# Two projections per matmul: 512-wide token-major projections, their weight loads on ScalarE's queue, four and four PSUM banks

## The chip, the cores and the metric

The kernel runs on one core of one Trainium2 chip. The metric is the device time of one execution in microseconds (us); a kernel is timed in several runs and the median counts. TensorE does matrix products into PSUM (eight banks of 2 KB per partition, 512 float32 columns each), VectorE and ScalarE do elementwise work and empty PSUM, GpSimd does elementwise work on SBUF alone, and SyncE (SP) issues most of the DMAs.

## What is computed

One decoder layer in float32 over 2048 tokens of width 1024. Every token is RMS-normalised and goes through one input projection; its columns feed four mLSTM heads (q and k of 128, v, o and z of 256 columns each) and eight gated DeltaNet heads (q, k, v and a gate z of 128 columns each); one output projection, a residual and a final RMSNorm follow.

```python
def reference(x, attn_norm, w_in, ...):
    h = rms_norm(x, attn_norm[l])
    proj = jnp.einsum('bsd,dp->bsp', h, w_in[l])
    (mq, mk, mv, mo, mz, mi, mf, gqkv, gz, gb, ga) = jnp.split(proj, split_points, axis=-1)
    h_m = mlstm_chunkwise(q_m, k_m, v_m, i_pre, f_pre)
    h_m = h_m * lax.rsqrt(jnp.mean(h_m * h_m, axis=-1, keepdims=True) + EPS)
    y_m = merge_heads(h_m) * m_out_norm[l] * jax.nn.sigmoid(mo) * jax.nn.silu(mz)
    qkv = jax.nn.silu(causal_depthwise_conv(gqkv, g_conv[l]))
    o_g = gated_delta_chunkwise(l2_norm(q), l2_norm(k), v, log_alpha, beta)
    o_g = o_g * lax.rsqrt(jnp.mean(o_g * o_g, axis=-1, keepdims=True) + EPS) * g_out_norm[l]
    y_g = merge_heads(o_g) * jax.nn.silu(gz)
    x = x + jnp.einsum('bsm,md->bsd', jnp.concatenate([y_m, y_g], axis=-1), w_out[l])
    return rms_norm(x, final_norm)
```

## The kernel before

**Segments and windows.** The 2048 tokens are worked on in four segments of `T` = 512, each in four chunks of 128 (`NCH`). A segment has eight windows: P0, M0, P1, M1, ... P3, M3 (`ORDER`; the last segment ends P2, P3, M2, M3). A P window projects two DeltaNet heads (`g_proj`), an M window one mLSTM head (`m_proj`).

**Projections.** Each weight group of 256 columns and its activations are split into a high and a low part, and every product is three matmuls (high-high, high-low, low-high). `proj_fm` (lines 348 to 358) is feature-major: the stationary operand is a 128x128 piece of weight, 512 tokens stream by; it serves q, k and the DeltaNet's q, k, v. `proj_tm` (lines 384 to 393, matmuls in `tm_step`, lines 360 to 365) is token-major: the stationary operand is a 128x128 piece of activations, and the 256 columns of one weight group stream by; it serves v, o and z of an mLSTM head (`pt_mv`, `pt_mo`, `pt_mz`) and the DeltaNet gate (`pt_gz`). A token-major group is four chunks of 8 x 3 matmuls, each chunk into a bank of its own.

**PSUM.** Three banks (`psj`, line 95) serve the projections, five (`psc`, line 96) everything else. An M window's v is emptied by ScalarE (high part, line 532) and VectorE (low part `vlo`, line 540), its z by ScalarE (tanh) and VectorE (lines 549 to 552).

**Weights.** SBUF holds ten units of 512 KB (half of a group's high or low part). In the first segment `split_w` loads the raw weights, splits them and keeps both parts in DRAM; later segments load them back from there. `next_w` fetches the following group's four units each time a group begins (line 161, on SP's queue). That queue works in order, and also carries the small transfers of the other streams: y rows out (lines 671, 1021), broadcast rows in (561, 750), the DeltaNet's 32x32 blocks through DRAM (841, 845, 856, 860).

**What runs beside the projections.** TensorE's order is written out by hand (`tc.manual_schedule`): `window` walks through a projection's steps (the filler) and at given fractions of the window puts in one step of another stream: `g_prep` (products of k and q, `kk`), `g_level` (block inverses: `zp`, `fp`, `zq`, `fq`), `g_chain` (per chunk `sp`, `vq`, then `su` and `op`) and `m_chunks` (per chunk `nd` and `up`). A window's length `WIN` is 41.6 us of filler; `LVP`, `CHP`, `CHM` hold the fractions. The other engines' order comes from a scheduler with priorities (`tc.high_priority`). In the first segment the projections use unnormalised activations (`raw`), and the outputs are scaled by `fm_out` (line 367).

**mLSTM key transposes.** `m_chunks` needs k token-major. Except for one head of the last segment, `to_tokens` (line 499) does it with 16 VectorE transposes of 32-row blocks per head (line 504).

Of the kernel before, what the change touches and what calls it, by code (L numbers as in the profile page):

```python
# [17 lines left out]
P = 128  # L18
# [11 lines left out]
LVP = (0.26, 0.3, 0.34, 0.4, 0.45)  # L30
# [3 lines left out]
CHM = (0.03, 0.11, 0.28, 0.45, 0.53, 0.7, 0.87, 0.95)  # L34
MW, MPR, VPR = ((0.07, 0.85), 200, 200)
# [23 lines left out]
MT = ((1, 1, 1, 1), (1, 1, 1, 1), (1, 1, 1, 0))  # L59
# [10 lines left out]
def hybrid_layer(  # L70
# [24 lines left out]
    psj = ctx.enter_context(tc.tile_pool(name="psj", bufs=3, space=PSUM))  # L95
    psc = ctx.enter_context(tc.tile_pool(name="psc", bufs=5, space=PSUM))
# [54 lines left out]

    def unit(ncol, dt, nm):
        return wp.tile([P, HK, ncol], dt, tag="wu", name=nm, bufs=10)

    def load_w(key, src, ncol, nm, between=None):

        if key in parts_d:
            his, los = ([unit(ncol, F32R, f"{p_}_{nm}_{i}") for i in range(2)] for p_ in ("whi", "wlo"))
            for i in range(2):
                for part, t_ in enumerate((his[i], los[i])):  # L160
                    nc.sync.dma_start(t_.bitcast(F32), parts_d[key][part, i])
            return his, los
        return split_w(key, src, ncol, nm, between)

    def split_w(key, src, ncol, nm, between):
# [18 lines left out]
        kept = parts_d[key] = ypool.tile([2, 2, P, HK, ncol], F32, tag=f"wd{nm}", name=f"wd{nm}")  # L184
        for i in range(2):
            for part, t_ in enumerate((his[i], los[i])):
                nc.sync.dma_start(kept[part, i], t_.bitcast(F32))
        return his, los

    wloads = []  # L190
    for seg in range(NSEG):
        for kind, n in ORDER_LAST if seg == NSEG - 1 else ORDER:
            for i in range(4) if kind == "M" else (3, 1, 0, 2) if n == 0 else (1, 0, 2, 3):
                nm, key = f"{kind}{seg}_{n}_{i}", (kind, n, i)
                if kind == "M":
# [7 lines left out]
    def prefetch_w(between=None):  # L203
        if wloads:
            wready.append(load_w(*wloads.pop(0), between))
# [38 lines left out]
    def rms_first():  # L244
        pc = psc.tile([P, T], F32, tag="cp", name="rcp0")[:, 0:NCH]
# [102 lines left out]
    def proj_fm(w, c0, nm, done):  # L348

        hi, lo = w  # L350
        ps = psj.tile([P, T], F32, tag="pj", name=f"pf_{nm}")
        for k in range(KT):
            nc.tensor.matmul(ps, lhsT=hi[k // HK][:, k % HK, c0:c0 + P], rhs=hh[k], start=(k == 0), stop=False)  # L353
            nc.tensor.matmul(ps, lhsT=hi[k // HK][:, k % HK, c0:c0 + P], rhs=hl[k], start=False, stop=False)  # L354
            nc.tensor.matmul(ps, lhsT=lo[k // HK][:, k % HK, c0:c0 + P], rhs=hh[k], start=False, stop=(k == KT - 1))  # L355
            if k == KT - 1:
                done(ps)
            yield 0.65

    def tm_step(ps, w, t, k):  # L360
        hi, lo = (p_[k // HK][:, k % HK, :] for p_ in w)
# [5 lines left out]
    def fm_out(dst, ps, scale=None):  # L367
# [16 lines left out]
    def proj_tm(w, nm, done, scaled=True):  # L384

        n = w[0][0].shape[-1]
        for t in range(NCH):
            ps = psj.tile([P, T], F32, tag="pj", name=f"pt_{nm}_{t}")[:, 0:n]
            for k in range(KT):
                tm_step(ps, w, t, k)  # L390
                if k == KT - 1:
                    tm_done(ps, t, done, scaled)
                yield 0.33

    def proj_tm_first(w, nm, done):

        n = w[0][0].shape[-1]
        pss = [psc.tile([P, T], F32, tag="cp", name=f"pt_{nm}_{t}")[:, 0:n] for t in range(NCH)]
        for k in range(KT):
            for t in range(NCH):  # L400
                tm_step(pss[t], w, t, k)
            if k == KT - 1:
# [105 lines left out]
    def m_proj(seg, n, r):  # L508
        s_ = f"{seg}_{n}"
        w = next_w()  # L510
# [6 lines left out]
        yield from proj_fm(w, 0, f"mq{s_}",  # L517
                           lambda ps: fm_out(qT, ps, DK ** -0.5))
        yield from proj_fm(w, P, f"mk{s_}", lambda ps: fm_out(kT, ps))
        w = next_w()  # L520
# [7 lines left out]
        def keep_v(ps, t):  # L528
# [12 lines left out]
        yield from proj_tm(w, f"mv{s_}", keep_v, False)  # L541
        w = next_w()
        yield from proj_tm(w, f"mo{s_}", lambda ps, t: nc.scalar.activation(
            G[:, t, :], ps, AF.Tanh, scale=rs0h[:, t:t + 1] if raw[0] else 0.5), False)
# [859 lines left out]
```

## Time and profile before

| | |
|---|---|
| median of 3 runs | 2281.76 us (2275.52 to 2284.42) |
| the profiled execution | 2285.25 us, span 2283.5 us |
| TensorE matmuls busy | 2210.1 us, 97% of the span, 14798 instructions |
| VectorE busy | 1842.6 us, 81% |
| ScalarE busy | 861.8 us, 38% |
| GpSimd busy | 797.3 us, 35% |
| mean granted TensorE clock | 0.985 of full speed |
| DMA | 409.19 MB, mean 179 GB/s |

The profile comes from one execution of the program, taken by the hardware profiler. Busy times of one engine overlap where its instructions are pipelined: a matmul's recorded duration is longer than the distance to the next one's start, so TensorE's pace is read from starts. "Idle before" is the time an engine stood still ahead of an instruction, with the instruction that released it.

### The profile page before, as it was taken

The page shows a single profiled execution, that of the slowest core. Times are in us where ns is not written, and L with a number is a line of the kernel's source. Part 1 is how long each engine was busy: PE and PEld are TensorE (multiplying, and loading weights), DVE is VectorE, ACT ScalarE, POOL GpSimd, SP SyncE. Part 2 cuts the span into 40 slices and gives each one's busy share as a digit, 9 for nine tenths or more (in the row PEclk, how much of TensorE's full clock was granted, in tenths as well). Part 3 has the DMA queues.
Part 4 walks back from the last instruction along what each step waited for, and adds up shares of the span by engine and source line. Part 5 has one row for each costly group of instructions (what it writes and reads, how often), then busy time and mean ns, then how long its engine had stood idle before and what let it go on. Part 6 is the DMA issues. An engine that isn't in the chain of part 4 may idle for free.

```text
span 2283.5 us, 41793 instructions
## 1 busy us (share of the span) xinstructions
PE 2210.1 (97%) x14798; PEld 1963.8 (86%) x14798; DVE 1842.6 (81%) x5168; ACT 861.8 (38%) x2289; POOL 797.3 (35%) x1220
## 2 busy tenths in 40 slices
PE   8899999989999999999999999999999999999998
PEld 7779898987989898988898989898988997788787
DVE  7988888788897979888979798788757737878784
ACT  5445454535343434352424243524244334111111
POOL 4657565652120202521212114212111115555543
PEclk9999999999999999999999999999999999999999
DMA  8767676764536464655454546544546545222321
GB/s 273 265 236 252 231 242 240 255 216 157 193 135 213 138 212 159 224 167 182 162 187 163 176 169 237 178 152 166 184 168 209 192 152 162 80 96 92 102 84 65
DMA packets 183322, 409.19 MB, mean 179 GB/s; under 512 B 51736, under 2 KB 84632, under 8 KB 183112
## 3 DMA queue, kind: packets, MB, share of 16 engines
q1 hardware_dynamic: 182392, 405.74, 52.4%
q8 instruction: 116, 1.90, 0.3%
q14 instruction: 94, 0.77, 0.1%
q10 hardware_dynamic: 720, 0.79, 0.1%
HBM read 309.68 MB, written 96.90 MB: 178 GB/s over the span
## 4 chain that ended last, share of the span: by engine, by line
PE 62%; DVE 25%; DMA 5%; ACT 4%; issue 2%; POOL 2%; SPq 0%; POOLq 0%; ACTq 0%; DVEq 0%
PE po L1260 5%; PE po L1259 5%; PE po L1258 5%; DVE tb L850 3%; DVE xb L854 3%; DVE kw L504 2%; PE pf_gv L355 2%; PE pf_gv L353 2%; PE pf_gv L354 2%; PE pt_gz L365 2%; PE pf_gq L353 2%; PE pt_gz L363 2%; PE pt_gz L364 2%; PE pt_mo L363 2%; PE pt_mo L364 2%
## 5 line engine op out<-in xcount | busy, mean ns | idle before, releaser
L1219 DVE STREAM_TRANSPOSE ytt<-yl 32x256 f32<-32x256 f32 x448 | 195.3, 436 | 45.3 <-POOL ylo L1187 39.2
L1016 POOL TENSOR_TENSOR gms<-gms,nhalf 128x2 f32<-128x2 f32 x64 | 46.7, 729 | 395.8 <-DVE gms L1014 386.5
L850 DVE TENSOR_TENSOR tb<-xb,lbt 128x248 f32<-128x248 f32 (+30 forms) x496 | 170.1, 343 | 17.8 <-DMA lbt<-l_d 5.0
L854 DVE TENSOR_TENSOR xb<-xb,tb 128x248 f32<-128x248 f32 (+30 forms) x496 | 167.7, 338 | 13.2
L363 PE MATMUL pt_mv<-whi_M,hh 128*128 128x256 f32 x512 | 152.7, 298 | 21.7 <-DVE vlo L540 14.6
L363 PE MATMUL pt_mz<-whi_M,hh 128*128 128x256 f32 x512 | 149.7, 292 | 7.6 <-DVE tz L550 7.5
L363 PE MATMUL pt_gz<-whi_P,hh 128*128 128x256 f32 (+1 forms) x512 | 149.7, 292 | 1.8 <-ACT whi_P L179 1.5
L364 PE MATMUL pt_mv<-wlo_M,hh 128*128 128x256 f32 x512 | 148.6, 290 | 0.1
L365 PE MATMUL pt_mv<-whi_M,hl 128*128 128x256 f32 x512 | 148.5, 290 | 0.0
L363 PE MATMUL pt_mo<-whi_M,hh 128*128 128x256 f32 x512 | 148.4, 290 | 0.0
L365 PE MATMUL pt_gz<-whi_P,hl 128*128 128x256 f32 (+1 forms) x512 | 146.7, 286 | 0.4 <-DVE hl L342 0.2
L364 PE MATMUL pt_gz<-wlo_P,hh 128*128 128x256 f32 (+1 forms) x512 | 146.4, 286 | 0.4 <-DVE wlo_P L182 0.4
L365 PE MATMUL pt_mz<-whi_M,hl 128*128 128x256 f32 x512 | 145.1, 283 | 0.0
L364 PE MATMUL pt_mz<-wlo_M,hh 128*128 128x256 f32 x512 | 145.1, 283 | 0.0
L364 PE MATMUL pt_mo<-wlo_M,hh 128*128 128x256 f32 x512 | 144.2, 282 | 0.0
L365 PE MATMUL pt_mo<-whi_M,hl 128*128 128x256 f32 x512 | 144.2, 282 | 0.0
L363 PEld LDWEIGHTS pt_mv<-whi_M,hh 128*128 128x128 f32 x512 | 101.4, 198 | 25.1 <-DVE vlo L540 16.0
L1267 ACT ACTIVATE jkf<-xr 128x512 f32<-128x512 f32 (+1 forms) x33 | 20.4, 619 | 271.5 <-DVE xr L1265 148.4
L1258 PE MATMUL po<-woh,yh 128*128 128x512 f32 (+1 forms) x297 | 114.6, 386 | 1.5 <-ACT yh L1185 1.5
L1260 PE MATMUL po<-woh,ylo 128*128 128x512 f32 (+1 forms) x297 | 114.9, 387 | 0.1
L1259 PE MATMUL po<-wol,yh 128*128 128x512 f32 (+1 forms) x297 | 114.3, 385 | 0.0
L182 POOL TENSOR_TENSOR wlo_M<-wraw_M,whi_M 128x256 fp32r<-128x256 f32 x128 | 98.4, 801 | 40.6 <-ACT whi_M L179 40.6
(407 smaller groups left out, 7541.7 us busy)
## 6 DMA issues: line engine op xcount, KB each, us to landing
whi_M<-wdM SPq DMA_DIRECT2D x96, 512.0 KB, 4.0
wlo_M<-wdM SPq DMA_DIRECT2D x96, 512.0 KB, 5.5
whi_P<-wdP SPq DMA_DIRECT2D x90, 512.0 KB, 4.7
wlo_P<-wdP SPq DMA_DIRECT2D x90, 512.0 KB, 6.0
wraw_M<-in_wg_dram SPq DMA_DIRECT2D x32, 512.0 KB, 5.8
wdM<-whi_M SPq DMA_DIRECT2D x32, 512.0 KB, 2.9
wdM<-wlo_M SPq DMA_DIRECT2D x32, 512.0 KB, 5.0
wraw_P<-in_wg_dram SPq DMA_DIRECT2D x30, 512.0 KB, 5.7
```

The lines of the kernel that those rows point to most:

```text
L182: eng.tensor_tensor(lo[:, ks, :], raw_[:, ks, :], hi[:, ks, :].bitcast(F32), op=ALU.subtract)
L353: nc.tensor.matmul(ps, lhsT=hi[k // HK][:, k % HK, c0:c0 + P], rhs=hh[k], start=(k == 0), stop=False)
L363: nc.tensor.matmul(ps, lhsT=hh[k][:, ts], rhs=hi, start=(k == 0), stop=False)
L364: nc.tensor.matmul(ps, lhsT=hh[k][:, ts], rhs=lo, start=False, stop=False)
L365: nc.tensor.matmul(ps, lhsT=hl[k][:, ts], rhs=hi, start=False, stop=(k == KT - 1))
L850: nc.vector.tensor_tensor(tb[:, :, 0:n], xb[:, :, i:i + 1].broadcast_to([P, 8, n]), lbt[:, i:i + 1, i + 1:32].broadcast_to([P, 8, n]), op= ...
L854: nc.vector.tensor_tensor(xs, xs, tb[:, :, 0:n], op=ALU.subtract)
L1016: nc.gpsimd.tensor_tensor(ms, ms, nhalf[:, 0:2], op=ALU.pow)
L1219: nc.vector.transpose(ytt[32 * b:32 * b + 32, :, 32 * a:32 * a + 32], y3[32 * a:32 * a + 32, :, 32 * b:32 * b + 32])
L1258: nc.tensor.matmul(ps, lhsT=yh, rhs=woh, start=(k == 0), stop=False)
L1259: nc.tensor.matmul(ps, lhsT=yh, rhs=wol, start=False, stop=False)
L1260: nc.tensor.matmul(ps, lhsT=ylo, rhs=woh, start=False, stop=(k == 15))
```

## The change

Five things change together.

- **Wide token-major projections** (`proj_tm_wide`). From the second segment on, o and z of an mLSTM head are projected together, 512 columns per matmul: two chunks at a time, each into a whole bank. For the DeltaNet gates of P1 to P3 (in the last segment of P1 alone) the gate leaves the P window and is projected in the M window that follows, together with v (`both`). The M window then begins with that pair, q and k come second. The fillers are 31.0 and 52.0 us long in such windows (`WINP`, `WINM`), with fractions of their own (`LVW`, `CWP`, `CWM`); the P window holds 4 chain steps instead of 5, the M window 9 instead of 8.
- **Weight units from ScalarE's queue.** From the second segment on, units are loaded by `pump`, called where the program frees a unit (`freed`), from ScalarE's queue; a wide group has eight units of two k-rows by 512 columns. The first segment's copies in DRAM are laid out 512 wide for the pairs.
- **Banks.** `psj` 4 instead of 3, `psc` 4 instead of 5. `rms_first` takes its bank from `psj`.
- **First segment's key transposes** go to TensorE (`MT`): 16 more transposes there, and where the products are split (`fast`) both parts are made from PSUM.
- **First segment's feature-major outputs** are scaled by one kind of VectorE instruction, with priority 200 (`VPR`).

```diff
-LVP = (0.26, 0.3, 0.34, 0.4, 0.45)
+NU = 10
+LVP, LVW = (0.26, 0.3, 0.34, 0.4, 0.45), (0.2, 0.24, 0.29, 0.34, 0.41)
 CHP = (0.42, 0.46, 0.63, 0.71, 0.88)
 CHM = (0.03, 0.11, 0.28, 0.45, 0.53, 0.7, 0.87, 0.95)
+CWP = (0.44, 0.5, 0.7, 0.82)
+CWM = (0.01, 0.15, 0.22, 0.36, 0.5, 0.57, 0.71, 0.85, 0.92)
...
-MT = ((1, 1, 1, 1), (1, 1, 1, 1), (1, 1, 1, 0))
+MT = ((0, 0, 0, 0), (1, 1, 1, 1), (1, 1, 1, 0))
...
-    psj = ctx.enter_context(tc.tile_pool(name="psj", bufs=3, space=PSUM))
-    psc = ctx.enter_context(tc.tile_pool(name="psc", bufs=5, space=PSUM))
+    psj = ctx.enter_context(tc.tile_pool(name="psj", bufs=4, space=PSUM))
+    psc = ctx.enter_context(tc.tile_pool(name="psc", bufs=4, space=PSUM))
...
+    ring = {"free": NU}
+    coming = []
+    def pump():
+        while coming and ring["free"] > 0:
+            w = coming[0]
+            at, src = w.due.pop(0)
+            t_ = w.units[at] = unit_(w.rows, w.n, F32R, f"w{at[0]}_{w.nm}_{at[1]}")
+            nc.scalar.dma_start(t_.bitcast(F32), src)
+            ring["free"] -= 1
+            if not w.due:
+                wready.append(coming.pop(0))
+    def freed(n):
+        ring["free"] += n
+        if not wloads:
+            pump()
...
+    WIDE = [[("M", n, 2), ("M", n, 3)] for n in range(4)] + [[("P", n, 3), ("M", n, 1)] for n in range(1, 4)]
+    def wide_z(seg, n):
+        return seg > 0 and n > 0 and not (seg == NSEG - 1 and n > 1)
...
+    def proj_tm_wide(w, nm, done):
+        for t0 in range(0, NCH, 2):
+            pss = [psj.tile([P, T], F32, tag="pj", name=f"pt_{nm}_{t0 + i}") for i in range(2)]
+            for k in range(KT):
+                for i in range(2):
+                    tm_step(pss[i], w, t0 + i, k)
+                    if t0 and i and k % 2:
+                        freed(2)
+                    if k == KT - 1:
+                        done(pss[i], t0 + i)
+                    yield 0.65
...
-        elif scale is None:
-            nc.vector.tensor_tensor(dst, ps, rbc0, op=ALU.mult)
         else:
-            nc.vector.scalar_tensor_tensor(dst, ps, scale, rbc0, op0=ALU.mult, op1=ALU.mult)
+            with tc.high_priority(VPR):
+                nc.vector.scalar_tensor_tensor(
+                    dst, ps, 1.0 if scale is None else scale, rbc0, op0=ALU.mult, op1=ALU.mult)
...
+        def gates(ps, t):
+            nc.scalar.activation(G[:, t, :], ps[:, 0:256], AF.Tanh, scale=0.5)
+            gate(ps[:, 256:512], t)
+        if wide_z(seg, n):
+            z_gate = g_gate(seg, n, rp, None)
+            def both(ps, t):
+                z_gate(ps, t)
+                keep_v(ps[:, 256:512], t)
+            yield from proj_tm_wide(next_w(), f"mv{s_}", both)
...
-        if fast or by_dve(MT, seg, h):
+        if by_dve(MT, seg, h) or not fast:
+            kw = sm.tile([P, NCH, P], F32, tag="kw", name=f"kw{s_}", bufs=1)
+        if by_dve(MT, seg, h):
             to_tokens(kT, kw)
...
+            if fast:
+                kw = ktp.rearrange("p (c f) -> p c f", c=NCH)
...
-    WIN = 41.6
+    WIN, WINP, WINM = 41.6, 31.0, 52.0
```

## Rows read from the trace of the kernel before

**Rows 1.** The page's first part: busy time, share and instructions of each engine.

```profile
PE 2210.1 (97%) x14798; PEld 1963.8 (86%) x14798; DVE 1842.6 (81%) x5168; ACT 861.8 (38%) x2289; POOL 797.3 (35%) x1220
```

**Rows 2.** Who waited for whom, TensorE: us in total, times, longest.

```profile
PE pt_mv L363 <- DVE vlo L540: 14.6, 7, 3.4
PE pt_mz L363 <- DVE tz L550: 7.5, 5, 3.1
PE vq L982 <- DVE vr L976: 4.8, 2, 3.8
...
PE pt_mv L363 <- DVE mk L375: 4.0, 2, 3.5
...
PE pt_mv L363 <- DVE vlo L537: 3.1, 2, 3.0
PE zp L910 <- DVE dmz L904: 3.0, 2, 1.8
PE sp L973 <- DVE ua L832: 2.4, 1, 2.4
```

**Rows 3.** Six stretches at half clock: busy by engine, PEclk, DMA share, GB/s.

```profile
1043.80:1050.60 6.80, 6.18 (x29) 6.18 (x30) 6.56 (x23) 3.54 (x10) 2.84 (x4) 0.50 0.49 152
...
sum 23.90, PE 23.02 PEld 22.73 DVE 19.78 ACT 8.75 POOL 5.32; mean PE 3.84 PEld 3.79 DVE 3.30 ACT 1.46 POOL 0.89
```

**Rows 4.** Timeline of TensorE, first and last of 62 matmuls of 256 columns.

```profile
702.97 0.28 PE L364 MATMUL pt_mo<-wlo_M,hh 128*128 128x256 f32 x1
...
710.22 0.28 PE L365 MATMUL pt_mo<-whi_M,hl 128*128 128x256 f32 x1
```

**Rows 5.** Timeline of TensorE, output projection, first and last of 45 matmuls.

```profile
1999.62 0.39 PE L1258 MATMUL po<-woh,yh 128*128 128x512 f32 x1
...
2009.79 0.40 PE L1260 MATMUL po<-wE,ylo 128*128 128x512 f32 x1
```

**Rows 6.** Timeline of TensorE around its longest wait for a bank.

```profile
1040.79 0.28 PE L365 MATMUL pt_mv<-whi_M,hl 128*128 128x256 f32 x1
1044.42 0.58 PE L363 MATMUL pt_mv<-whi_M,hh 128*128 128x256 f32 x1 [3.35 <-DVE vlo L540]
```

**Rows 7.** Timeline of VectorE in the same stretch.

```profile
1038.66 3.16 DVE L504 STREAM_TRANSPOSE gv<-xingv 32x128 f32<-32x128 f32 x10
...
1043.95 0.42 DVE L540 TENSOR_TENSOR vlo<-pt_mv,mv 128x256 fp32r<-128x256 f32 x1
```

**Rows 8.** SP's queue waiting to load units: longest and shortest of seven rows.

```profile
SPq L161 <- PE pf_gq L355: 157.7, 22, 15.4
...
SPq L161 <- PE pt_gz L365: 40.0, 23, 3.8
```

**Rows 9.** A P window, its gate, the M window behind it: busy by engine.

```profile
726.50:783.30 56.80, 56.80 (x406) 49.21 (x405) 49.73 (x139) 27.18 (x75) 10.38 (x23) 1.00 0.50 165
783.30:839.70 56.40, 54.59 (x418) 52.33 (x417) 46.34 (x165) 15.14 (x47) 9.82 (x14) 1.00 0.52 184
...
771.40:783.30 11.90, 11.90 (x102) 11.90 (x101) 11.66 (x33) 7.34 (x28) 4.39 (x6) 1.00 0.39 123
```

**Rows 10.** VectorE's groups of instructions in the first segment: the key transposes.

```profile
L504 DVE STREAM_TRANSPOSE kw<-mk 32x128 f32<-32x128 f32 x64 | 19.4, 302 | 1.0
```

**Rows 11.** The last segment's one head transposed on TensorE (ns min/median/max).

```profile
L601 PE MATMUL ktp<-ident,mk x4: 272/273/273, 1887.0 to 1887.3; 128*128 128x128 f32 x4
L603 DVE TENSOR_SCALAR kw<-ktp,ws x4: 341/342/351, 1887.6 to 1888.4; 128x128 f32<-128x128 f32 x4
```

**Rows 12.** Line 671 on ScalarE's queue: four DMA issues (ns min/median/max).

```profile
L671 ACTq DMA_DIRECT2D yd<-yt x4: 326/326/342, 1896.0 to 1924.3; - x4
```

**Rows 13.** Timeline of TensorE: first and last writes to `psc` tiles, 762.6 to 771.1.

```profile
762.64 0.28 PE L620 MATMUL nd<-mv,pts 128*128 128x258 f32 x1
...
771.08 0.28 PE L620 MATMUL up<-mv,kws_pt 128*128 128x258 f32 x1
```

**Rows 14.** Timeline of VectorE: the last reader of the older of them.

```profile
772.26 0.48 DVE L667 SCALAR_TENSOR_TENSOR yt<-nd,mr,mg 128x256 f32<-128x256 f32 x1
```

More of the change, by code (lines that the diff above doesn't have):

```diff
@@ L150, in hybrid_layer, with unit_, __init__, part @@
     parts_d = {}
+    def unit_(rows, ncol, dt, nm):
+        return wp.tile([P, rows, ncol], dt, tag="wu", name=nm, bufs=NU)
     def unit(ncol, dt, nm):
[L153 to L158, printed above, removed]
-            for i in range(2):
[L160 to L163, printed above, removed]
+        return unit_(HK, ncol, dt, nm)
+    class Weights:
+        def __init__(self, nm, ncol, rows):
+            self.nm, self.n, self.rows, self.units, self.due = nm, ncol, rows, {}, []
+        def part(self, p_, k):
+            return self.units[p_, k // self.rows][:, k % self.rows, :]
+    ring = {"free": NU}
+    coming = []
+    def get_w(key, nm):
+        if isinstance(key, list):
+            w = Weights(nm, 512, 2)
+            kept = parts_d[key[0]][0]
+            w.due = [((p_, i), kept[p_, i // 2, :, i % 2 * 2:i % 2 * 2 + 2]) for i in range(4) for p_ in range(2)]
+        else:
+            kept, c0, n = parts_d[key]
+            w = Weights(nm, n, HK)
+            for i in range(2):
+                for p_ in range(2):
+                    w.due.append(((p_, i), kept[p_, i, :, :, c0:c0 + n]))
+        return w
+    def pump():
[11 more added lines that the diff above has]
+            pump()
     def split_w(key, src, ncol, nm, between):
@@ L204, in prefetch_w @@
         if wloads:
-            wready.append(load_w(*wloads.pop(0), between))
+            wready.append(split_w(*wloads.pop(0), between))
+            if not wloads:
+                coming.extend(get_w(*g_) for g_ in wgets)
+                ring["free"] = NU - 8
     def next_w():
@@ L360, in tm_step @@
     def tm_step(ps, w, t, k):
-        hi, lo = (p_[k // HK][:, k % HK, :] for p_ in w)
+        hi, lo = (w.part(p_, k) for p_ in range(2))
         ts = slice(t * P, (t + 1) * P)
@@ L390, in proj_tm @@
                 tm_step(ps, w, t, k)
+                if t == NCH - 1 and k % HK == HK - 1:
+                    freed(2)
                 if k == KT - 1:
@@ L716, in g_proj_z, with g_gate @@
     def g_proj_z(seg, pr, r, st):
+        gate = g_gate(seg, pr, r, st)
+        yield from (proj_tm_first if seg == 0 and pr == 0 else proj_tm)(next_w(), f"gz{seg}_{pr}", gate)
+    def g_gate(seg, pr, r, st):
         s_ = f"{seg}_{pr}"
-        w = next_w()
         G = wkp.tile([P, NCH, 256], F32, tag="gg", name=f"gg{s_}", bufs=2)
@@ L734, in gate @@
                     beta[:, t, :], ps[:, 272:280], -1.0, 85.0, op0=ALU.mult, op1=ALU.min)
-        yield from (proj_tm_first if seg == 0 and pr == 0 else proj_tm)(w, f"gz{s_}", gate)
+        return gate
     def g_prep(seg, pr, r, st):
```

89 lines of the change are left out of this document (58 added, 31 removed).

## Prediction

> **What bounds the kernel now.** The page's busy shares come first: TensorE is at 97%, VectorE at 81%, ScalarE at 38% [rows 1]. TensorE executes an order written by hand, so the time can only fall where its stream gets shorter or stands still less. Two readings follow from that.
>
> The first is its pace, read from starts. In a quiet stretch 62 matmuls of 256 columns start from 702.97 to 710.22, so 61 steps of 118.9 ns [rows 4]. In the output projection 45 matmuls of 512 columns, with activations stationary and weights streaming as the changed projections have them, start from 1999.62 to 2009.79, 44 steps of 231.1 ns [rows 5]. Two narrow ones cost 237.7 ns, one wide one 231.1: the streamed columns cost nearly all, the number of instructions little.
>
> The second is the list of waits. TensorE waits for VectorE, and the largest rows are all a token-major group that wants a bank still being emptied: 14.6 us for `vlo` (7 times), 7.5 for `tz` (5 times), 4.0 for `mk`, 3.1 for the first segment's `vlo`; together 29.2 us in 16 waits [rows 2]. The longest shows the mechanism. TensorE stops at 1040.79 and goes on at 1044.42 [rows 6]; VectorE spends that time on ten transposes of `gv` from 1038.66 and other work, and reaches `vlo` at 1043.95 [rows 7]. VectorE isn't short of time there, its order is wrong by some 3 us, and three banks don't cover that. After such a stop the granted clock falls to half: six stretches that stand behind waits for banks last 23.9 us together [rows 3], and half of that is lost.
>
> **The change, part by part.** The sum is made against the profiled execution, 2285.25 us, which lies 3.5 above the median of the runs shown (2281.76).
>
> *Wide projections.* 12 groups of o with z (4 heads, 3 segments) and 7 of gate with v (three in each of segments 1 and 2, one in the last) make 19, each of 4 chunks x 8 k-steps x 3 products = 96 pairs: 1824 pairs x 6.6 ns [rows 4, 5] = -12.0 us. The bounds are 0 (the stream is all that counts) and -20, had the two paces each been misread by 2 ns. The Trainium skill's page "TensorE: Matmul & The Clock Gate", section "Back-to-back issue gap", gives N/2.4 + 2.5 ns, by which a pair saves 2.5 ns and the 1824 save 4.6 us; by that the sum below ends 7 us higher. Both measured paces lie above that formula, by 9.7 and 15.3 ns, and the rows decide.
>
> *Waits for banks.* A wide pair of chunks occupies TensorE for 48 x 0.231 = 11.1 us while two other banks are emptied, where before two narrow chunks (5.7 us) were the cover. All o and z groups after the first segment are wide, so no wait for `tz` should stay there. What stays narrow (the first segment, and v in M0 and in the last segment) gets a fourth bank, 24 x 0.119 = 2.9 us more cover, against waits of at most 3.0 to 3.5 us [rows 2]. Of 29.2 us I keep 3: -26. Bounds: -29 and -15, if the fourth bank is taken up by VectorE falling further behind.
>
> *The clock.* If those stops go, so do the slow stretches behind them: half of 23.9 us is 12 [rows 3]; I take -10, between 0 and -12.
>
> *First segment.* VectorE loses 64 transposes, 19.4 us [rows 10]. In the one head whose products aren't split, four multiplications of 0.34 us come back, and TensorE gets 16 transposes; the four starts of the trace lie within 0.3 us [rows 11], so 16 cost 1.8 us, at most 16 x 0.272 = 4.4. What VectorE's free time can give back are waits for `vr`, `dmz` and `ua` (4.8, 3.0 and 2.4 us [rows 2]); at 10.2 us these are the bound, and I take -2, as 19.4 us are spread over four M windows and these waits come from latency. The output scaling is one VectorE instruction either way; its priority is part of the bank waits above (`mk`). `rms_first` in another bank and the 1 KB runs of the DRAM copies cost nothing: nobody on TensorE waits for those writes until a segment later, and if that cover were gone, it would show as a wait for `whi` in P1 of segment 1.
>
> *One `psc` bank fewer.* In the trace of before, a new `psc` tile is now and then begun while four are open. Between 762.64 and 771.08 TensorE writes `nd`, `vq`, `su`, `op`, `nd` and begins `up` [rows 13]; the first `nd` is read last at 772.26 to 772.74 [rows 14], and of the others only `vq` is done. With four banks `up` starts 1.7 us late. I take such a place to exist in every P window of segments 1 and 2 behind the first and in each M0 window, where `kk` tiles come thick. From nothing (the new fractions may move the steps apart) to 2 us in each of some eleven windows, 22 us: I take +9, between the two.
>
> *ScalarE's queue.* 384 loads (32 groups x 4 units x 3 segments) leave SP. SP stood 532 us waiting to issue them, in seven rows from 157.7 down to 40.0 [rows 8], with small transfers queued behind it; these now go earlier. TensorE has no wait for a DMA among its rows, so I give no gain. An issue costs ScalarE 0.326 us [rows 12], 125 us in all, which fits beside 38% busy. But in ScalarE's order each load waits for TensorE's last reading of its unit, and what stands behind it (emptying a bank, the copies in `g_level` that TensorE needs a step later) waits too. Program order puts the load right where the unit is freed, so the wait is the distance by which ScalarE is ahead, and what remains is two issues, 0.7 us, now and then ahead of a copy that TensorE needs. From 0 to 20 us (some 30 of the 192 pairs of loads): +4.
>
> *Windows.* The gate moves out of seven P windows. Such a window is 56.8 us long, 11.9 of them the gate, and has 49.73 us of VectorE work; the M window behind it has 46.34 in 56.4 [rows 9]. The P window shrinks to 44.9 us and keeps nearly all of VectorE's work (the convolutions and transposes): VectorE is over by 4.8 us, less the gate's own instructions and one chain step. The M window grows by as much and has 10 us to spare, so most can slide. From 0 to 7 x 4.8 = 34 us: +5.
>
> **Sum.** 2285.25 - 12.0 - 26 - 10 - 2 + 1.8 + 9 + 4 + 5 = 2255; against the median, 3.5 lower: **2252 us**.
>
> **Rivals.**
> - *VectorE becomes the bound of the short P windows.* For it: 49.73 us of work against 44.9 [rows 9]; the two `xin` buffers of the convolution tie a projection's bank to VectorE's progress, and the missing `psc` bank adds to it. Against: VectorE already defers transposes into the M window. If all 34 us are lost, 2252 + 29 = 2281: no change.
> - *ScalarE takes over SP's waits* (slower). The place is ScalarE's order: a load that isn't ready holds back the bank behind it. The Trainium skill says on the same page, under "Architectural detail", that ScalarE's queue is strict first-in first-out; no row here shows a ready instruction held there. If a tenth of the 532 us [rows 8] reaches TensorE, +53: 2305. It decides from 42 us on, 8% of them. Against it: SP's loads stood in the queue from the start of a group, ScalarE's come where the unit is freed.
> - *More comes back than I count*: `psc`, ScalarE and the windows cost nothing and the first segment's other waits go too: 2252 - 18 - 8 = 2226.
> - *The pairs save nothing* (columns alone count): 2264, inside the forecast's range.
>
> **How the numbers follow.** About 0.5% (11 us) is what a measurement of this kernel can tell from no change. Forecast 0.62, with a range of its own of 2234 to 2270, all of it faster; more than counted 0.10, faster; VectorE-bound windows 0.16, around 2281, of which 0.03 faster, 0.11 the same, 0.02 slower; ScalarE 0.12, of which 0.11 slower and 0.01 the same. That makes faster 0.75, same 0.12, slower 0.13. The range for 8 in 10 reaches from just above the third rival to the first: 2229 to 2283.
>
> **What would show it.** In the profile after: `pt_mo` and `pt_mv` as 128x512 at 231 ns from start to start (wide step wrong if 238 or more); no wait for `tz` after the first segment and none for `vlo` over 1 us; fewer stretches at half clock; waits of `kk`, `up` or `su` for VectorE's or ScalarE's last reader of a `psc` tile, under 2 us each (the `psc` term); P windows of some 45 us from `pf_gk` to the wide group with VectorE near full and no wait of `pf_gq` or `pf_gv` for a bank (if such waits sum to 30 us, the first rival holds); loads on ScalarE's queue, with ScalarE's copies in `g_level` as prompt as before (if TensorE waits for `dmz` or `E` in every window, the second). The forecast is wrong if the waits move to another bank pool instead of going away.

## The result and the profile after

The changed kernel takes 2340.24 us (median of 4 runs, 2338.26 to 2350.47), the kernel before beside it 2283.09: ratio 1.0252, 95% interval 1.0234 to 1.0271. It is slower by 57 us where 30 us of gain were forecast. The profiled execution's span is 2336.5 us, its mean granted clock 0.977 of full speed (before 0.985).

The page's first part after, to be held against [rows 1]:

```profile
PE 2215.2 (95%) x12990; PEld 1884.1 (81%) x12990; DVE 1838.1 (79%) x5108; ACT 852.6 (36%) x2289; POOL 813.1 (35%) x1219
```

1808 matmul instructions fewer (1824 pairs became single ones, 16 transposes came in), and no engine's share is higher: nobody is the new bound, TensorE stands still more (span less busy time: 73.4 us before, 121.3 after). The pace of the wide matmuls, from TensorE's timeline in an o and z group (first and last of 27):

```profile
830.96 0.39 PE L430 MATMUL pt_mo<-w_M,hh 128*128 128x512 f32 x1
...
836.94 0.39 PE L432 MATMUL pt_mo<-w_M,hl 128*128 128x512 f32 x1
```

26 steps in 5.98 us are 230.0 ns each; two narrow ones cost 237.7 [rows 4]. A pair saves 7.7 ns, 1824 of them 14 us of TensorE's stream. That much of the forecast holds. Now who TensorE waited for (us in total, times, longest), the answer to [rows 2]:

```profile
PE zp L1016 <- DVE dmz L1010: 17.3, 8, 7.4
PE op L1104 <- DVE ua L938: 12.4, 6, 2.4
PE zq L1036 <- DVE dmz L1031: 11.9, 7, 1.9
PE nd L720 <- DVE CN L753: 9.9, 6, 3.6
PE kk L927 <- DVE SS L1112: 7.9, 2, 5.9
...
PE fp L1025 <- ACT dmz L1020: 6.2, 3, 2.9
```

The 29.2 us that projections waited for a bank are gone but for 1.3 us (for `tz`). In their place stand the other streams: the steps of the block inverses (`zp`, `fp`, `zq`) wait 35.4 us, before 3.0 + 4.5 + 4.3 = 11.8; `op` and `kk` wait 20.3 us for a `psc` bank whose last reader (`ua`, `SS`) is late. The clock went the wrong way too. With two levels, 1.2 and 2.4 GHz, a mean of 0.985 means 2 x 0.015 x 2283.5 = 69 us at half clock before, 0.977 means 2 x 0.023 x 2336.5 = 107 us after; half of the difference, 19 us, is lost.

The windows that the change reshaped, P2 and M2 of the second segment (length, then busy us of PE, PEld, DVE, ACT, POOL, granted clock, DMA share, GB/s), answer to [rows 9]:

```profile
736.70:786.50 49.80, 47.11 (x305) 38.75 (x304) 40.26 (x112) 22.93 (x64) 11.66 (x23) 0.97 0.46 148
786.50:855.30 68.80, 66.82 (x325) 56.10 (x324) 57.31 (x192) 18.48 (x59) 10.38 (x16) 0.98 0.54 182
```

118.6 us for the pair against 113.2 before. The short window lasts 49.8 us instead of the 44.9 that the forecast counted (56.8 - 11.9), and VectorE is busy in 40.26 of them, 81%. It isn't over, as the forecast's term and its first rival had it.

### The profile page after: what moved, and what is told of

It is laid out like the page before. It is cut to its first block, busy times and chain, and to the rows that moved or that the text cites. A ratio compares the mean times of both kernels' runs of the same rounds, so it can differ in the third digit from the quotient of the medians.

```text
span 2336.5 us, 38095 instructions
## 1 busy us (share of the span) xinstructions
PE 2215.2 (95%) x12990; PEld 1884.1 (81%) x12990; DVE 1838.1 (79%) x5108; ACT 852.6 (36%) x2289; POOL 813.1 (35%) x1219
## 5 line engine op out<-in xcount | busy, mean ns | idle before, releaser
L430 PE MATMUL pt_mo<-w_M,hh 128*128 128x512 f32 x384 | 156.8, 408 | 0.0
L432 PE MATMUL pt_mo<-w_M,hl 128*128 128x512 f32 x384 | 151.2, 394 | 0.0
L431 PE MATMUL pt_mo<-w_M,hh 128*128 128x512 f32 x384 | 151.0, 393 | 0.0
L220 POOL TENSOR_TENSOR wlo_P<-wraw_P,whi_P 128x256 fp32r<-128x256 f32 x104 | 88.7, 881 | 58.4 <-ACT whi_P L217 57.2
L1334 POOL TENSOR_TENSOR ytt<-ytt,gain_c 128x256 f32<-128x256 f32 x120 | 82.9, 721 | 69.6 <-DVE ytt L1331 69.6
L803 DVE SCALAR_TENSOR_TENSOR gk<-xingk,conv_c,gk 128x512 f32<-128x512 f32 x96 | 74.6, 778 | 23.7 <-ACT gk L800 21.2
L430 PE MATMUL pt_mv<-w_V,hh 128*128 128x512 f32 x224 | 91.7, 409 | 0.0
L1299 POOL TENSOR_TENSOR ylo<-ytt,yh 128x256 fp32r<-128x256 f32 x120 | 85.1, 746 | 16.1 <-ACT yh L1297 16.1
L589 DVE STREAM_TRANSPOSE gv<-xingv 32x128 f32<-32x128 f32 x288 | 87.1, 302 | 4.3
L589 DVE STREAM_TRANSPOSE ktok<-gk 32x128 f32<-32x128 f32 x288 | 87.1, 302 | 4.2
L431 PE MATMUL pt_mv<-w_V,hh 128*128 128x512 f32 x224 | 88.7, 396 | 0.0
L432 PE MATMUL pt_mv<-w_V,hl 128*128 128x512 f32 x224 | 88.6, 396 | 0.0
```

The costliest lines, as they stand in the source:

```text
L220: eng.tensor_tensor(lo[:, ks, :], raw_[:, ks, :], hi[:, ks, :].bitcast(F32), op=ALU.subtract)
L430: nc.tensor.matmul(ps, lhsT=hh[k][:, ts], rhs=hi, start=(k == 0), stop=False)
L431: nc.tensor.matmul(ps, lhsT=hh[k][:, ts], rhs=lo, start=False, stop=False)
L432: nc.tensor.matmul(ps, lhsT=hl[k][:, ts], rhs=hi, start=False, stop=(k == KT - 1))
L589: nc.vector.transpose(dst[32 * a:32 * a + 32, :, 32 * b:32 * b + 32], s4[32 * b:32 * b + 32, :, a, :])
L1299: eng.tensor_tensor(ylo[:, ks], yt_[:, ks], yh[:, ks].bitcast(F32), op=ALU.subtract)
```

## The experiments

Every ratio is to the kernel before on the same chip; 0.001 is 2.3 us. The theories were: (A) the `psc` pool, a bank poorer, takes over the waits; (B) the loads on ScalarE's queue are the cost, either because SP's small transfers come late beside them or because they stand in ScalarE's order; (C) the moved gate with its short P windows is. A fourth came up on the way: that VectorE's amount of work is what TensorE meets wherever it gets ahead.

### One part undone at a time

**Loads from SP's queue again** (changed kernel):

```diff
-            nc.scalar.dma_start(t_.bitcast(F32), src)
+            nc.sync.dma_start(t_.bitcast(F32), src)
```

> The changed kernel with one edit: the units are begun from SP's queue at the same places of the program. Theory A (the loss is the psc bank: TensorE's waits for op, kk and sp on the last readers of older psc tiles, some 29 us, and the half-clock stretches behind them): 2340 us within 8, those waits stay. Theory B (the loads on a queue of their own, beside SP's, make the small transfers late: VectorE's waits for lbt and E rose from 13 to 75 us, and TensorE's waits in g_level from 12 to 35): about 2310, the waits for lbt and E back under 25 us and zp's wait (17.3) under 6. Theory C (the shortened P windows with the gate moved: steps stand closer than their predecessors take): 2340 within 8, the zq waits of 2.0 us per window stay.

Measured: 2317.65 us, ratio 1.0136 (1.0114 to 1.0157), so 0.0116 or 26 us come back, with some 7 us of uncertainty, as in every difference of two such ratios. But not by the way of late transfers: VectorE's waits for `lbt` and `E`, the blocks that go through DRAM, sum to 74.8 us in the changed kernel and 72.4 here (13.4 before).

**Three and five banks again** (changed kernel; `psj` 3, `psc` 5):

```diff
-tc.tile_pool(name="psj", bufs=4, space=PSUM)
+tc.tile_pool(name="psj", bufs=3, space=PSUM)
-tc.tile_pool(name="psc", bufs=4, space=PSUM)
+tc.tile_pool(name="psc", bufs=5, space=PSUM)
```

> The changed kernel with three banks for the projections and five for the rest. Theory A: the waits of op for ua (12.4 us), kk for SS and ktok (11.9) and sp for ua (2.4) go, some 40 us with the clock; what the wide pairs then wait for a third and fourth bank comes on top, up to 2 us in each of 38 places, so 2300 to 2360. Theories B and C: the waits in g_level (35 us) stay as they are; if none of A's waits goes, A is wrong; with the new bank waits of the pairs 2350 to 2410.

Measured: 2382.04 us, 1.0415 (1.0396 to 1.0435). TensorE's waits in this run:

```profile
PE pt_mv L430 <- DVE vlo L621: 32.3, 6, 7.9
PE pt_mo L430 <- DVE tz L625: 21.8, 7, 6.8
```

The wide pairs hold two banks at a time and need the fourth; with it taken away they wait more than the narrow groups ever did; `op` waiting for `ua` is no longer among the largest rows, for `psc` has its fifth bank back.

**The gate back in the P windows** (changed kernel; o and z stay wide):

```diff
-        return seg > 0 and n > 0 and not (seg == NSEG - 1 and n > 1)
+        return False
```

> The changed kernel with the gate left in every P window (so 41.6 us windows with the old fractions, v narrow); o with z stay wide. Theory C: the zq waits of 2.0 us and the waits of op for ua (one of 2.2 us in each wide M window) go with their clock stretches, about 2300 us. Theory A: the waits on psc readers stay in other places, 2330 to 2345. Theory B: VectorE's waits for lbt and E stay above 50 us, 2330 to 2345.

Measured: 2313.18 us, 1.0106 (1.0080 to 1.0133): 0.0146 or 33 us come back.

**Four and four banks alone** (kernel before):

```diff
-psj = ... bufs=3        psc = ... bufs=5
+psj = ... bufs=4        psc = ... bufs=4
-        pc = psc.tile([P, T], F32, tag="cp", name="rcp0")[:, 0:NCH]
+        pc = psj.tile([P, T], F32, tag="pj", name="rcp0")[:, 0:NCH]
```

> The kernel before with one part alone: four and four banks (rms_first's tile moved to the projections' pool, as in the change). Theory A: the 29 us of waits of the projections fall to under 5, and new waits on psc readers of 30 us or more come, with half-clock stretches: 2290 to 2325 us. Theories B and C: the projections' waits go, little comes back: 2245 to 2270.

Measured: 2291.43 us, 1.0027 (1.0011 to 1.0043). This is the run that meets the forecast's largest terms by themselves, and they fall: the waits for `vlo` and `tz` are gone but for 3.4 us and the time is 6 us longer. Its largest waits:

```profile
PE up L620 <- DVE yt L667: 11.0, 6, 2.3
PE vq L982 <- DVE vr L976: 6.8, 5, 3.1
PE fp L919 <- ACT dmz L914: 5.9, 3, 2.3
PE zp L910 <- DVE dmz L904: 4.2, 2, 2.5
```

`up` waits for the last reader of `nd`, the place that the forecast had found [rows 13, 14]; the other rows have grown from 4.8, 4.5 and 3.0 us. All of TensorE's waits in this list sum to 65.9 us in the kernel before and to 74.6 here.

**Two parts undone** (both edits together, SP's queue and the gate in the P windows):

```diff
-            nc.scalar.dma_start(t_.bitcast(F32), src)
+            nc.sync.dma_start(t_.bitcast(F32), src)
...
-        return seg > 0 and n > 0 and not (seg == NSEG - 1 and n > 1)
+        return False
```

> The changed kernel with two parts undone at once: the units are loaded from SP's queue, and the gate stays in the P windows, so that only o with z is wide. Alone these two gave back about 23 and 27 us. If they are separate costs (the order of ScalarE's work; the short P windows), they add up: 2290 us, give or take 6, ratio about 1.003, which is the time of the kernel before with its banks shared four and four. If they are one cost seen twice (both only relieve the P windows), most of the second gain is gone: 2305 to 2313. Below 2280 the forecast's gains from wide pairs and fewer waits would be there after all, hidden under those two parts.

Measured: 2291.27 us, 1.0024 (1.0009 to 1.0039). The two costs add up: by their sum the ratio would be 1.0252 - 0.0116 - 0.0146 = 0.9990, and all but 0.0034 (8 us) of that is there, a rest that the intervals allow. Against the two runs with one part undone, the second one gives 26 us for the gate (from 1.0136) and 19 us for the queue (from 1.0106).

**The first segment's parts undone too** (these two edits and two more; left are the banks, the wide o and z, and `pump`, which begins a unit's load as soon as the unit is free):

```diff
-MT = ((0, 0, 0, 0), (1, 1, 1, 1), (1, 1, 1, 0))
+MT = ((1, 1, 1, 1), (1, 1, 1, 1), (1, 1, 1, 0))
...
+        elif scale is None:
+            nc.vector.tensor_tensor(dst, ps, rbc0, op=ALU.mult)
         else:
-            with tc.high_priority(VPR):
-                nc.vector.scalar_tensor_tensor(
-                    dst, ps, 1.0 if scale is None else scale, rbc0, op0=ALU.mult, op1=ALU.mult)
+            nc.vector.scalar_tensor_tensor(dst, ps, scale, rbc0, op0=ALU.mult, op1=ALU.mult)
```

> As the run beside it (SP's queue, gate in the P windows), and also the first segment's VectorE work and the output scaling as in the kernel before: what is left of the change is four and four banks, o with z as 512 wide pairs, and units begun when one comes free. By the forecast's terms the 12 wide groups save 1152 x 7 ns = 8 us on top of what four and four banks alone gave (2291): 2283. If TensorE's saved time only turns into waits for VectorE, it stays at 2288 to 2295. If the first segment's edit and the priority of the scaling are worth the forecast's 2 us or nothing, this run and the one beside it agree within 6 us; if TensorE's new transposes cost more than was counted, this one is the faster by more.

Measured: 2295.13 us, 1.0035 (1.0020 to 1.0051). With four and four banks, 12 wide groups, whose matmuls need 9 us less, and `pump` together gained nothing over the run with the banks alone. No run undoes `pump` by itself.

### Is it VectorE's amount of work?

Both kernels with this edit, which leaves out two of the convolution's three multiply-adds:

```diff
-                    for tap in range(3):
+                    for tap in range(1):
```

> The changed kernel with two of the three multiply-add taps of the convolution's loop left out (its result is then another one; about 190 us of VectorE's work go, and nothing of TensorE's). If the amount of VectorE's work is what turns the removed waits into others, TensorE's saved time now shows: this runs at or below the kernel before with the same cut, by up to the forecast's 30 us. If it is the order on ScalarE and the places of the windows, whatever VectorE has to do, most of the 57 us between the two kernels stays: 35 us or more above the kernel before with the same cut. Between (10 to 35): both have a part.

> The kernel before with the same two taps left out. TensorE is busy 97% of it, so it can fall by little: if its waits come from VectorE's amount of work, to 2230 to 2255 us; if from the order of VectorE's work, it stays above 2265. It is the base for the run beside it.

Measured: changed 2340.75 us, 1.0238 (1.0217 to 1.0260); before 2311.99 us, 1.0108 (1.0087 to 1.0129). With VectorE's work cut by 134 us (1842.6 to 1708.8) the kernel before became 25 us slower, and the changed one stayed where it was, 29 us above it. The page's busy line of the cut kernel before, and the row of its waits that grew most:

```profile
PE 2213.8 (96%) x14798; PEld 1964.8 (85%) x14798; DVE 1708.8 (74%) x4976; ACT 861.0 (37%) x2289; POOL 764.9 (33%) x1220
```

```profile
PE fp L919 <- ACT dmz L914: 19.3, 10, 3.7
```

That wait was 4.5 us in the kernel before. The scheduler that orders the other engines made a new order for the smaller work, and the hand-written order of TensorE meets it less well. The longest of these waits, 3.70 us at 1107.97, shows it. VectorE's timeline ahead of it, and at the same place of the kernel before:

```profile
1099.93 5.04 DVE L504 STREAM_TRANSPOSE ktok<-gk 32x128 f32<-32x128 f32 x16
1105.01 0.69 DVE L585 TENSOR_TENSOR pts<-ptt,pts 128x512 fp32r<-128x512 f32 x1
```

```profile
1090.11 0.69 DVE L585 TENSOR_TENSOR pts<-ptt,pts 128x512 fp32r<-128x512 f32 x1
1090.71 5.04 DVE L504 STREAM_TRANSPOSE ktok<-gk 32x128 f32<-32x128 f32 x16
```

With less work, 16 transposes stand ahead of `pts`; ScalarE waits 3.99 us for it, and `dmz`, which `fp` needs, comes behind that in ScalarE's order. The amount theory finds no support: less work gave back nothing in either kernel, and at the place shown TensorE waits for where an instruction stands in another engine's order.

An attempt to mend that order directly, in the kernel before:

```diff
-MW, MPR, VPR = ((0.07, 0.85), 200, 200)
+MW, MPR, VPR = ((0.07, 0.85), 200, 1000)
...
-            nc.vector.scalar_tensor_tensor(tz, tz, 1.0, ps, op0=ALU.add, op1=ALU.mult)
+            with tc.high_priority(VPR):
+                nc.vector.scalar_tensor_tensor(tz, tz, 1.0, ps, op0=ALU.add, op1=ALU.mult)
```

> The kernel before, with three and five banks and narrow projections, and with a higher priority in VectorE's order for three instructions alone: the scaling of the feature-major projections, vlo, and the first instruction on tz. If the forecast's reading of those waits was right (29 us of TensorE's time and 24 us at half clock that only the emptying of three banks costs), they fall and the time with them: 2250 to 2270 us. If a wait that is taken away here comes back at the next instruction that VectorE now does later (vr, ua, dmz, yt), the waits for vlo and tz fall and the time stays: 2275 to 2292.

Measured: 2285.61 us, 1.0002 (0.9989 to 1.0014). The waits for `vlo` and `tz` stayed (14.6 and 7.2 us), so the priority changed nothing there and the run decides nothing.

### Is `psc` short?

`su` and `op` of a chunk in one bank, in three versions (with loads on SP's queue in all):

```diff
+            so_ = psc.tile([P, 512], F32, tag="cp", name=f"su{n_}")
             if not last:
-                su = psc.tile([P, 512], F32, tag="cp", name=f"su{n_}")
+                su = so_[:, 0:256]
...
-            op_ = psc.tile([P, 512], F32, tag="cp", name=f"op{n_}")
+            op_ = so_[:, 256:512]
```

> The changed kernel with SP's queue and the gate in the P windows (2291 us), and with su and op of a chunk, 256 columns each, in one psc bank in place of two. If the missing fifth psc bank is what eats the gain (up waiting for yt 10.1 us, kk for SS and ua 5.5, sp for ua 3.0 in that run), these waits fall and the time comes to 2268 to 2278, below the kernel before. If they are only where VectorE's order is late, they move on and it stays at 2286 to 2296. One bank for two tiles also has a price: VectorE reads su only when op is done, a few tenths of a us on the chain, which could make it the slower by up to 6 us.

> The kernel before with four and four banks (2291 us) and su and op in one psc bank. As in the run beside it: psc as the cause 2268 to 2280, with up waiting for yt (11.0 us in six waits) mostly gone; VectorE's order 2286 to 2296. Against the run beside it, this one tells what the wide groups of o with z are worth once psc isn't short: by the forecast's pairs 8 us.

> The changed kernel with SP's queue (2318 us), the gate in the M windows as changed, and su and op in one psc bank. If the moved gate costs its 27 us through psc (op waiting for ua, the reader of kk, in every shortened window), much of it goes: 2285 to 2300. If the short P windows cost it through latencies that no bank covers (E and dmz late for the levels), it stays at 2310 to 2320.

Measured: with o and z wide and the gate in place 2281.11 us, 0.9982 (0.9968 to 0.9997); kernel before with four and four banks 2293.40 us, 1.0035 (1.0022 to 1.0049); with the gate moved 2319.26 us, 1.0150 (1.0134 to 1.0165). In the first, `up`'s wait for `yt` falls from 10.1 us to none and 10 us come back. In the second the same wait goes from 11.0 us to none and nothing comes back; TensorE's waits sum to 73.4 us, after 74.6. And the moved gate costs 0.0168, 38 us, with the pool relieved in this way: that shortage of `psc` isn't its cause. Between the second and the first lie 12 us; by the pairs the wide o and z should give 9, but the two versions differ in `pump` and the first segment's parts too.

The squares of k, summed by ScalarE, written into SBUF in place of a bank:

```diff
-            tp = psc.tile([P, 512], F32, tag="cp", name=f"ktp{s_}_{j}")
+            if by_dve(KTR, seg, pr):
+                tp = None
+            else:
+                tp = psc.tile([P, 512], F32, tag="cp", name=f"ktp{s_}_{j}")
...
-                    nc.scalar.activation(tp[:, c * P:(c + 1) * P], kt_[:, c, :], AF.Square,
+                    nc.scalar.activation(ua[j][:, c, 0, :], kt_[:, c, :], AF.Square,
```

> The version with SP's queue, the gate in the P windows and su and op in one bank (2281 us), and with ScalarE's sums of the squares of k writing their unused squares into SBUF in place of a psc bank. If psc is still short in it (kk waiting for ua 5.4 us, sp for ua 7.3), 2268 to 2276; if not, 2278 to 2284.

Measured: 2277.01 us, 0.9962 (0.9949 to 0.9974), 5 us below the version that it starts from. With the first segment's `MT` row back to ones:

> The best version so far (2277 us) with the transposes of kw in the first segment back on VectorE. By the forecast's terms (-2 and +1.8) nothing: 2273 to 2281. If VectorE is what holds the first segment up, 2284 or more; if TensorE's 16 transposes and the waits around them cost more than was counted, 2270 or less.

Measured: 2274.57 us, 0.9956 (0.9942 to 0.9970). The two intervals overlap: the first segment's edit is worth nothing that these runs can tell, as forecast, and this is the fastest version that was run. TensorE's waits sum to 65.0 us in it, about as much as in the kernel before (65.9): its 10 us are about what 1152 pairs save (9), and none of the runs above has a sum clearly below the kernel before.

### What the moved gate costs

The level's steps are placed at fractions of the window, and the change made the window shorter and the fractions smaller. TensorE's timeline with the gate in place (su and op in one bank): start of the P window, then `zp`, `fp` and `zq`.

```profile
726.56 0.40 PE L418 MATMUL pf_gk<-hh,w_P 128*128 128x512 f32 x1
...
741.43 0.69 PE L1016 MATMUL zp<-dmz,ua 32*32 32x32 f32 x32
743.64 0.69 PE L1025 MATMUL fp<-E,dmz 32*32 32x32 f32 x32
747.35 1.14 PE L1036 MATMUL zq<-dmz,ua 64*64 64x64 f32 x16
```

The same with the gate moved:

```profile
737.57 0.40 PE L418 MATMUL pf_gk<-hh,w_P 128*128 128x512 f32 x1
...
746.90 0.69 PE L1016 MATMUL zp<-dmz,ua 32*32 32x32 f32 x32
749.11 0.69 PE L1025 MATMUL fp<-E,dmz 32*32 32x32 f32 x32
753.97 1.14 PE L1036 MATMUL zq<-dmz,ua 64*64 64x64 f32 x16 [1.88 <-DVE dmz L1031]
```

`zp` comes 9.3 us into the window instead of 14.9, and `zq` is due before VectorE has turned the block that it needs. VectorE there, in the second run:

```profile
751.21 0.93 DVE L589 STREAM_TRANSPOSE ktok<-gk 32x128 f32<-32x128 f32 x3
752.15 0.35 DVE L713 SCALAR_TENSOR_TENSOR kws_nm<-kw,ws,kws_pt 128x128 fp32r<-128x128 f32 x1
752.52 0.93 DVE L589 STREAM_TRANSPOSE ktok<-gk 32x128 f32<-32x128 f32 x3
753.48 0.43 DVE L1031 STREAM_TRANSPOSE dmz<-E 32x256 f32<-32x256 f32 x1
```

ScalarE had written the block, two copies from 750.25 lasting 0.77 us, by 751.02; VectorE reached it 2.5 us later, behind transposes of `ktok` and splits of `kw` (with the gate in place 1.7 us later). In that run `zq` waits 14.4 us in 8 places, with the gate in place 5.5 in 4. Put back at the distances, in units of matmul time, that the kernel before has:

```diff
-LVW = (0.2, 0.24, 0.29, 0.34, 0.41)
+LVW = (0.35, 0.403, 0.456, 0.537, 0.604)
-CWP = (0.44, 0.5, 0.7, 0.82)
+CWP = (0.565, 0.616, 0.845, 0.95)
-CWM = (0.01, 0.15, 0.22, 0.36, 0.5, 0.57, 0.71, 0.85, 0.92)
+CWM = (0.108, 0.227, 0.292, 0.427, 0.563, 0.627, 0.763, 0.9, 0.963)
```

> The changed kernel with SP's queue and su and op in one bank (2319 us), and with the steps of the levels and of the chain put at the same distances from the start of the P window, in matmul time, as in the kernel before (the first level step 10.8 units in, in place of 6.2; the last two 2.8 apart, in place of 2.2). If the places of the steps are what the moved gate costs, zq's waits for dmz, 2.04 us in each of six windows, and zp's go, and the half clock behind them: 2285 to 2300. If the loss comes from VectorE having less time in the P window whatever the places, the waits move on to the chain (vq, su, sp): 2312 to 2325.

Measured: 2299.06 us, 1.0062 (1.0042 to 1.0082). Of the 38 us, 20 come back by an edit of the places alone; `zq`'s waits fall to 1.7 us, `zp`'s from 7.0 to 3.8, and the mean clock rises from 0.977 to 0.984. Not all of it need be the distance to VectorE's work: with the gate moved TensorE also waited 12.1 us for weight units that came late (`pf_mq` 7.0 of them, in six places), and in this run it doesn't wait for any. The remaining 18 us are not settled; the largest new row of that run is `sp` waiting for `SS`, 17.3 us in six places, and why it came isn't shown.

### What ScalarE's queue costs

The version of 2277 us, with the loads on ScalarE's queue:

```diff
-            nc.sync.dma_start(t_.bitcast(F32), src)
+            nc.scalar.dma_start(t_.bitcast(F32), src)
```

> The best version so far (gate in the P windows, su and op in one bank, the squares of k in SBUF; 2277 us), with the units loaded from ScalarE's queue as the change does. If ScalarE's queue costs by itself, as the sum of the single undoings said, 2295 to 2305; if it cost only together with the moved gate and the short bank pool, within 6 us of 2277.

Measured: 2299.67 us, 1.0083 (1.0055 to 1.0111) against 0.9962: 28 us, where the pair with the moved gate gave 26 and the pair with the gate back 19. Late transfers aren't it here either: VectorE's waits for `lbt` and `E` are 55.3 us, with SP's queue 52.5. Two runs of the changed kernel were to tell issuing from holding. In the first, each load goes to SP's queue and a transfer of 64 bytes is issued from ScalarE's beside it:

```diff
-            nc.scalar.dma_start(t_.bitcast(F32), src)
+            nc.sync.dma_start(t_.bitcast(F32), src)
...
+            nc.scalar.dma_start(scr[i_:i_ + 1, :], src[0:1, 0, 0:16])
```

> The changed kernel with the units loaded from SP's queue (2318 us), and beside each load a transfer of 64 bytes between two places in DRAM, issued from ScalarE's queue at the same place in the program, with nothing to wait for. If it is the issuing that costs ScalarE (384 x 0.326 us = 125 us of its time), the time goes back to that of the changed kernel: 2335 to 2345. If it is that a load not yet allowed to start holds what stands behind it, it stays within 6 us of 2318.

Measured: 2514.64 us, 1.1004 (1.0976 to 1.1033), which neither side had expected. The small transfers' groups (ns min, median, max; first and last start) show why:

```profile
L196 ACTq DMA_DIRECT2D scr<-wdP x228: 475/489/3677, 16.1 to 620.4; - x114
L196 ACTq DMA_DIRECT2D scr<-wdM x156: 475/476/3510, 94.4 to 675.0; - x156
```

With nothing later to wait for, all 384 were ordered into the first segment, behind the DRAM copies that they read. The run doesn't measure what was meant. It does show ScalarE standing behind transfers in its own queue (`mg` 19.9 us in five places for one of `scr`).

In the other run loads enter the program 4.4 us later (a list of freed units, counted down by the filler's steps):

```diff
+            late.append([LATE, n])
...
+    def tick(cost):
+        for l_ in late:
+            l_[0] -= cost
+        while late and late[0][0] <= 0:
+            ring["free"] += late.pop(0)[1]
+            pump()
```

> The changed kernel, loads on ScalarE's queue as changed, but each pair of loads enters the program 3.25 units of matmul time (about 4.4 us) after its unit was last read. If loads that wait for TensorE's last reading hold ScalarE's work, ScalarE no longer meets them early, and most of the 23 us comes back: 2318 to 2328, less what later weights cost. If the issuing itself costs, or the place among ScalarE's other work, 2335 to 2350.

Measured: 2334.03 us, 1.0220 (1.0197 to 1.0242), some 7 us better than the changed kernel, hardly more than the intervals leave open, and between the two outcomes that were expected. ScalarE's timeline in that run shows a load that still stands between two pieces of its work:

```profile
1809.97 0.60 ACT L985 ACTIVATE qtp<-gq 128x512 f32<-128x512 f32 x1
1814.71 0.81 ACTq L193 DMA_DIRECT2D w_M<-wdM  x2
1815.56 0.60 ACT L985 ACTIVATE qtp<-gq 128x512 f32<-128x512 f32 x1 [4.99 <-DVE xb L972]
```

The same place with the loads on SP's queue (the 2277 us version):

```profile
1766.41 0.60 ACT L976 ACTIVATE qtp<-gq 128x512 f32<-128x512 f32 x1
1768.34 0.60 ACT L976 ACTIVATE qtp<-gq 128x512 f32<-128x512 f32 x1 [1.33 <-DVE qs L977]
```

Two loads stand between the two squares of q, and the second square comes 5.6 us after the first, not 1.9; the row names another releaser for the 4.99 us, but the loads' issue ends just ahead of the square, at 1815.52. The later place in the program didn't move them in ScalarE's order here. The Trainium skill's page "TensorE: Matmul & The Clock Gate" ("Architectural detail") gives ScalarE's queue a strict first-in first-out order, and these rows agree with it, without showing that the square was ready while the loads waited. Nor is all of the 5.6 us theirs. With SP's queue the second square was released by VectorE's reading of the first (`qs`); here VectorE does that later:

```profile
1813.12 0.70 DVE L986 TRANSPOSE_TENSOR_REDUCE qs<-qtp 128x16 f32<-128x512 f32 x1
```

If the square waited for that again, the loads held it for 1.7 us, from 1813.82 to 1815.56. That isn't yet the price. TensorE's longest stop near that place, with the loads on ScalarE in the version of 2299.67 us:

```profile
1783.23 0.40 PE L420 MATMUL pf_mk<-hh,w_M 128*128 128x512 f32 x1
1790.92 0.28 PE L1019 MATMUL zp<-dmz,ua 32*32 32x32 f32 x2 [7.29 <-DVE dmz L1013]
```

`zp` stands 7.3 us because VectorE's solve ends late: its 31 steps start from 1745.94 to 1785.74, 39.8 us, and with SP's queue from 1730.30 to 1763.83, 33.5 us, both seen in VectorE's timeline. The first step had waited for a transfer, and behind the last VectorE waits for the solved blocks' way through DRAM:

```profile
1745.94 0.42 DVE L959 TENSOR_TENSOR tb<-xb,lbt 128x248 f32<-128x248 f32 x1 [1.82 <-DMA lbt<-l_d]
1790.34 0.43 DVE L1013 STREAM_TRANSPOSE dmz<-E 32x256 f32<-32x256 f32 x1 [4.22 <-DMA E<-e_d]
```

Between its late steps stand eight scalings of `ktok`, 2.77 us, which with SP's queue came when all its steps had started. None of these rows names ScalarE, so how the 28 us divide between issuing, holding and a new order of the other engines stays open.

## Why the prediction was wrong

- **Wide projections, -12: right in size, as TensorE's stream.** 230.0 ns a step; 14 us of TensorE's time. In the kernel's time it came out only where no new wait ate it: nothing in the run with 12 wide groups over the banks alone, about 10 us in the fastest version. The formula that the forecast took from the Trainium skill's page "TensorE: Matmul & The Clock Gate" ("Back-to-back issue gap") is given there for a single matmul by itself, and makes an estimate of 215.8 ns for 512 columns. The trace doesn't agree, and the rows were the better guide.
- **Waits for banks, -26, and the clock, -10: the steps that failed first.** Their reading was right, the waits for `tz` and `vlo` did go. But the forecast counted a wait that is taken away as time won. With the banks alone the time rose by 6 us where these terms with the `psc` term (-26 - 10 + 9) say -27. The waits moved, as the forecast's last sentence has it: 11.0 us to `up` in the other pool. But relieving that pool there gave nothing either: `sp`, `zq` and `fp` then waited 7.7, 7.3 and 6.7 us, where they had waited 4.0, 3.7 and 5.9. In sum TensorE waited 65.9 us before, 74.6 with the banks, 73.4 with the relief, and 114.2 in the changed kernel. The clock went with the waits: 19 us more lost in the changed kernel in place of 10 won.
- **One `psc` bank fewer, +9: the place right.** Its relief was worth 10 + 5 us in the version with wide o and z; in the one without, only the first of the two was tried, and it gave nothing.
- **ScalarE's queue, +4 (0 to 20): mis-sized.** 26, 28 and 19 us by three pairs of runs, at its bound of 20 or over it. The second rival had the side and priced 53; its way, a load that holds what stands behind it, isn't shown to be the price.
- **Windows, +5 (0 to 34): mis-sized, and for the wrong reason.** 33, 38 and 26 us by three pairs. VectorE was not over in the window shown (40.26 of 49.8 us). 20 of the 38 us came back with the steps' places: a P window shortened by the gate brings `zp` 5.5 us closer to the work that feeds it. The forecast costed the moved work and not the steps whose places are fractions of the window; [rows 9] can't show that, the two lists in the diff do.
- **First segment, -2 and +1.8: right**, no difference that the runs can tell.

The miss is 88 us: 33 in banks and clock, 22 in ScalarE's queue, 28 in the windows; 5 are left over, less than the uncertainty of one such difference.

## What to carry to other kernels

Where one engine's order is written by hand and the others' are made by a scheduler, a wait on the hand-ordered engine can be worth less than its length (here 29 us of waits went and nothing came back): remove it alone, run that, and only then add the next. When a window is shortened, compute each placed step's distance from the work that feeds it, before and after. Of two queues for loads that must wait for a buffer, time both: here 384 loads cost 19 to 28 us more on the queue of an engine that also computes, and the runs don't say by which way.

## What the runs showed that was not expected

- Less work can be slower: 134 us less on VectorE cost the kernel before 25 us.
- A part's worth depends on its company: one bank for `su` and `op` gave 10 us in the version with wide o and z and nothing in the kernel before with four and four banks.
- 384 transfers of 64 bytes from ScalarE's queue, ordered into the first segment, made the kernel some 197 us longer than the same kernel without them (2514.64 against 2317.65 us).
